# A two-layer three-mixer trunk: another order of the projections, and neighbouring query blocks paired in the weights-by-values products

## The chip, the cores and the metric

The kernel runs on one core of a Trainium2 chip, in one launch. The time is the device time of one execution in microseconds (us), the median of several. The engines are named as in the profile: PE is TensorE's matrix multiplication, PEld its loading of weights, DVE is VectorE, ACT is ScalarE, POOL is GpSimd and SP is SyncE, which here issues most DMAs.

## The reference

The input is 512 rows of 1024 values, ahead of which 16 learned meta rows are set, so 528 positions. Two layers follow, and each does this (cut to what matters):

```python
h = rmsnorm(x) ; proj = h @ w_in        # about 8400 columns, split into the inputs below
# A: stick-breaking attention, 8 heads of 64
# B: latent attention, 8 heads: q and k from low-rank codes, softmax, v of 64
# C: differential attention, 4 heads: (softmax1 - lam * softmax2) @ v, v of 128, then RMSNorm
y_sb, y_mla, y_diff = [(o * silu(z)) @ w_o for each branch]
merged = sum(sigmoid(gate logits) * y for the three branches)
x = x + merged @ w_out
```

Softmax is taken in query blocks of 128 positions. In B and C block j sees the keys of blocks 0 to j and 64 more, in A a query sees the keys before it. After the second layer comes a last RMSNorm, and the meta rows are dropped.

## The kernel before, in words

All products are done with float32 operands split in a high and a low part of a faster 4-byte type (H and L): one product is three matmuls, H by H, H by L and L by H (`mm3`, line 408). So nearly each operand passes a split: ACT copies the high part (line 430), DVE subtracts it (line 435, `low`), and PE waits for both.

The program is laid out at build time by a planner in the kernel (`Builder`). Each piece of work is a task, a Python generator that tells the engine of its next step; the planner keeps a planned time for each engine, takes the step that can start first, and writes its instructions down. The chip then runs each engine's instructions in that order: an engine that waits holds back everything written behind it. The projections, which make up most of PE's work, are one task of lowest priority (`products`): it goes through a list of items in a fixed sequence, and the attention's tasks are written down between its matmuls. An item can start when its weights are split and its condition holds; most conditions ask for memory (`room`).

The sequence is a string per layer, `ORDER`. Its letters: Q, q, k are the projections of A's queries and keys, V its values; C are B's codes; D i is the query and key projection of head i of C (two items, `dqk_item`, each with a rotation on DVE), U its values (`v_item`, item names dv); W and M are B's values and queries and keys; x, y, z are the gated paths of A, C, B; g and G are gate logits that are computed early and parked in DRAM (tensor g_d); s, m, d are the output projections of the branches A, B, C, where each `y` item (`y_item`) loads two parked gate logits from g_d and adds to a running sum in DRAM (acc_d), which the first two branches store and the last two load. `load_x` and `wo_items` close the layer: the product with w_out.

Memory is one pool of 33 double pages. An item that finds too few pages free waits, and with it all items behind it.

The softmax of a head of B or C runs as blocks j = 3, 2, 1, 0 and, in layer 0, -1 for the meta rows (`sm_block`). A block is: scores on PE (`z`, shapes of 264, 400, 272, 144 columns), maximum on DVE (lines 1155 and 1157), exponential with a sum on ACT, reciprocal, and normalising on DVE (for C a TENSOR_SCALAR of line 444 and a SCALAR_TENSOR_TENSOR of line 439), transposition on PE (line 414, one matmul per key block), split by ACT and DVE into the slabs H and L. When all blocks of a head of C are there, `diff_av` does weights by values; for B `mla_av` does it for two heads and two of the four blocks at a time. In both, a pair of query blocks that needs the same key block is one step of 256 columns, and a block that needs a key block alone is one of 128. Blocks are paired as 0 with 2 and 1 with 3.

Of the kernel before, what the change touches and what calls it, by code (L numbers as in the profile page):

```python
# [18 lines left out]
T = 528  # L19
META = 16  # L20
# [10 lines left out]
HOP = dict(T=190.0, A=110.0, V=290.0, S=100.0, G=150.0)  # L31
PE_LATE = 100.0
ORDER = (
    "Q0 G14 G15 G00 V0 q1 g23 G27 k1 g26 C0 g05 Q2 V1 g13 Q3 g20 g22 g21 U0 D0 D1 U1 g16 D2 g24 x0 g01 D3 g25 g03 g17 g06 g07 W0 g12 M0 x2 x1 s9 g02 x3 s0 M1 y0 s1 g04 M2 s2 y1 W1 g10 z1 y3 M3 m9 d9 y2 z0 d2 s3 z2 g11 z3 m3 d1 d0 m2 m1 m0 d3",
    "Q0 G15 V0 G03 q1 G27 G23 k1 g26 Q2 C0 g05 V1 g22 g13 Q3 g21 g20 U0 D0 g12 D1 U1 g16 D2 g01 g24 g14 x0 g07 D3 g00 x2 g17 W0 M0 g25 x1 s9 x3 g02 g06 s0 M1 s1 g04 s3 s2 M2 z0 z2 W1 y0 y1 z3 M3 d9 y2 g10 y3 g11 z1 m9 d2 m3 d0 m2 m1 m0 d1 d3",
)
SB_AHEAD = 3
FINE = 80
# [316 lines left out]
class Builder:  # L355
# [765 lines left out]
    def sm_block(self, st, j):  # L1121

        nc = self.nc
        l, kind = st["l"], st["kind"]
# [59 lines left out]
        if kind == "d":  # L1184
            yield "T", both(lambda: st.get("ptfree"), lambda: self.P.can(2 if j == 3 else 1) if self.o_used == 0 else None)
            self.o_used += 1
            tb = self.P.alloc(2 if j == 3 else 1)
            tf = tb.flat()
            self.transposes(tf, P[0], j)
            P[0].free()  # L1190
            H, L = [s[j % 2].flat()[:, 416 if j > 1 else 0:][:, 0:w] for s in st["pt"]]
            yield from self.split(H, L, tf[:, 0:w])
            tb.free()
            self.o_used -= 1
            self.sm_left(st)
            return
        e, at = j % 2, 416 if j > 1 else 0
        for us in [(0, 1)] if j < 3 else [(0,), (1,)]:
            yield "T", both(lambda: self.P.can(2) if self.o_used == 0 else None, lambda: self.R.can(*[2, 2] * sum((e, u) not in st for u in us)))
            self.o_used += 1  # L1200
            tb = self.P.alloc(2)
            for i, u in enumerate(us):
                if (e, u) not in st:
                    st[e, u] = (self.R.alloc(2), self.R.alloc(2))
                self.transposes(tb.flat()[:, 512 * i:], P[u], j)
                P[u].free()
            left = Latch(len(us), lambda: (tb.free(), self.o_free()))
            for i, u in enumerate(us):
                H, L = [s.flat()[:, at:at + w] for s in st[e, u]]
                self.spawn(self.sm_turned(st, e, H, L, tb.flat()[:, 512 * i:512 * i + w], left), f"m{l}{st['u']}{j}")  # L1210

    def o_free(self):
        self.o_used -= 1

    def sm_turned(self, st, e, H, L, src, left):
        yield from self.split(H, L, src)
        left()
        st["n", e] = st.get(("n", e), 0) + 1
        if st["n", e] == 4:
            self.spawn(self.mla_av(st, e), f"m{st['l']}{st['u']}{e}")  # L1220

    def mla_av(self, st, e):

        yield "T", lambda: self.P.can(1)
        ps = self.P.alloc(1, True)
        for u in range(2):
            h = st["u"] * 2 + u
            vo = 128 * (h % 4)
            o = ps.v()[:, 256 * u:256 * u + 256].rearrange("p (a n) -> p a n", n=128)
            for bi in range(e + 4):  # L1230
                v = st["V"][h // 4][bi].v()
                H, L = [s.flat() for s in st[e, u]]
                if bi < e + 2:
                    H, L = [t[:, 0:832].rearrange("p (a n) -> p a n", n=416)[:, :, 128 * bi:128 * bi + 128] for t in (H, L)]
                    self.mm(o, v[:, vo:vo + 128], H, bi == 0 and u == 0, False)
                    self.mm(o[0:64], v[:, vo:vo + 64], L, False, False)
                else:
                    H, L = [t[:, 416 + 128 * bi:544 + 128 * bi] for t in (H, L)]
                    self.mm3(o[0:64, 1], v[:, vo:vo + 64], v[:, vo + 64:vo + 128], H, L, False, bi == e + 3)
        for u in range(2):  # L1240
            for s in st[e, u]:
                s.free()
        od = st["oslab"].v()
        q = [od[64 * u:64 * u + 64, META:T].rearrange("p (a b n) -> p b a n", b=2, n=128)[:, e] for u in range(2)]
        o = [ps.v()[:, 256 * u:256 * u + 256].rearrange("p (a n) -> p a n", n=128) for u in range(2)]
# [65 lines left out]
    def diff_av(self, st):  # L1311
# [3 lines left out]
        ps = self.P.alloc(1, True)  # L1315
        V = st["V"][h // 2]
        vo = 128 * (h % 2)
        pv = ps.v().rearrange("p (a b n) -> p b a n", b=2, n=128)
        for bi in range(5):
            j0 = max(0, bi - 1)  # L1320
            v = V[bi].v()
            for u in (0, 1):
                a0 = 0 if u >= j0 else 1
                if u + 2 < j0:
                    continue
                H, L = [t[u].flat()[:, 0:1056] for t in st["pt"]]
                if a0 == 0:
                    H, L = [t[:, 0:832].rearrange("p (a n) -> p a n", n=416)[:, :, 128 * bi:128 * bi + 128] for t in (H, L)]
                else:
                    H, L = [t[:, 416 + 128 * bi:544 + 128 * bi] for t in (H, L)]  # L1330
                self.mm3(pv[:, u, :, :] if a0 == 0 else pv[:, u, 1, :], v[:, vo:vo + 128], v[:, 256 + vo:256 + vo + 128],
                         H, L, bi == 0 and u == 0, bi == 4)
        st["ptdone"]()
        parts = st["slabs"][0]
        for s in st["slabs"][1:]:
# [11 lines left out]
        for a2, b2 in self.qr(l):  # L1347
            m = b2 - a2
# [854 lines left out]
```

## Time and profile before

| what | us |
|---|---|
| median of 3 runs (1365.02 to 1368.45) | 1368.17 |
| the profiled execution, its own time | 1365.92 |
| its span, first to last instruction | 1364.2 |
| PE busy | 1325.5 |
| DVE busy | 1002.8 |
| ACT busy | 831.2 |

PE is busy for 97% of the span, with 9506 matmuls, so time is lost or won where PE idles and in the number and width of its matmuls. A matmul's own duration in the profile (some 280 ns for 256 columns) overlaps with its neighbours'; what one costs in a stream is the distance from one start to the next. The mean granted clock of PE is 0.991 of 2.4 GHz.

### The profile page before, as it was taken

What the parts mean: (1) busy time and instruction counts of PE and PEld (TensorE: products, weight loads), DVE (VectorE), ACT (ScalarE), POOL (GpSimd) and SP (SyncE); (2) the same over time, 40 slices, a digit from 0 to 9 for tenths busy, and PEclk for the clock granted to TensorE, in tenths of its full rate; (3) what the DMA queues carried; (4) which work ended last, traced back from release to release, by engine and by line L of the source; (5) the groups of instructions that cost most, each with busy time, mean ns of one, the idle gap of its engine ahead of it and who ended that gap; (6) DMA issues with size and microseconds to landing.
All of it is one profiled execution on the core that took longest, in us unless ns stands there. A gap on an engine that the chain in (4) does not pass through costs nothing.

```text
span 1364.2 us, 25553 instructions
## 1 busy us (share of the span) xinstructions
PE 1325.5 (97%) x9506; PEld 1234.8 (91%) x9506; DVE 1002.8 (74%) x2318; ACT 831.2 (61%) x2003; POOL 111.4 (8%) x232
## 2 busy tenths in 40 slices
PE   9999999969999999999999999999999999999996
PEld 8999999969999999999998889898888888888886
DVE  7877866787776776857776678577977867676664
ACT  6678688555665665645557587574645656455352
POOL 0111012000000102000001120020000110110000
PEclk9999999989999999999999999999999999999998
DMA  4431323313233434248733423233242345423861
GB/s 156 127 116 59 116 75 108 104 48 93 80 115 116 122 106 128 74 163 303 230 110 102 117 74 103 94 93 117 63 131 83 108 122 173 127 79 108 288 236 63
DMA packets 67613, 164.73 MB, mean 121 GB/s; under 512 B 8792, under 2 KB 15320, under 8 KB 67488
## 3 DMA queue, kind: packets, MB, share of 16 engines
q1 hardware_dynamic: 59488, 149.21, 33.5%
q0 software_dynamic: 7168, 13.12, 4.7%
q8 instruction: 75, 1.23, 0.4%
q10 hardware_dynamic: 832, 0.76, 0.2%
q14 instruction: 50, 0.41, 0.1%
HBM read 124.39 MB, written 25.56 MB: 110 GB/s over the span
## 4 chain that ended last, share of the span: by engine, by line
PE 83%; DVE 9%; ACT 4%; DMA 2%; issue 1%; SPq 0%; POOL 0%; DVEq 0%; ACTq 0%; POOLq 0%
PE banks L405 80%; ACT page L430 4%; DVE page L435 4%; PE banks L414 3%; DVE page L439 2%; DVE wl L435 1%; DMA wr<-in_ws_dram 1%; ACT wh L430 1%; DMA page<-page 0%; DVE mx L1157 0%; DVE mx L1155 0%; DMA page<-g_d 0%; DVE page L444 0%; DVE page L449 0%; SPq L457 0%
## 5 line engine op out<-in xcount | busy, mean ns | idle before, releaser
L405 PE MATMUL banks<-hH,wh 128*128 128x256 f32 (+3 forms) x1272 | 402.3, 317 | 0.0
L405 PE MATMUL banks<-hL,wh 128*128 128x256 f32 (+3 forms) x1272 | 396.9, 313 | 0.0
L405 PE MATMUL banks<-hH,wl 128*128 128x256 f32 (+2 forms) x1240 | 388.9, 314 | 0.0
L405 PE MATMUL banks<-page,wh 128*128 128x256 f32 (+2 forms) x1708 | 357.4, 306 | 1.1 <-ACT wh L430 1.0
L430 ACT ACTIVATE wh<-wr 128x256 fp32r<-128x256 f32 (+2 forms) x524 | 237.4, 487 | 144.0 <-PE banks L405 102.2
L430 ACT ACTIVATE page<-page 128x272 fp32r<-128x272 f32 (+19 forms) x486 | 248.5, 531 | 115.3 <-DVE page L435 76.5
L430 ACT ACTIVATE page<-banks 128x272 f32<-128x272 f32 (+21 forms) x493 | 224.1, 465 | 155.2 <-PE banks L405 114.7
L435 DVE TENSOR_TENSOR wl<-wr,wh 128x256 fp32r<-128x256 f32 (+2 forms) x522 | 260.8, 516 | 57.8 <-ACT wh L430 55.1
L405 PEld LDWEIGHTS banks<-page,wh 128*128 128x128 f32 x1708 | 276.9, 190 | 15.4 <-ACT wh L430 2.1
L435 DVE TENSOR_TENSOR page<-page,page 128x256 f32<-128x256 f32 (+15 forms) x429 | 232.8, 558 | 63.7 <-ACT page L430 51.1
L405 PE MATMUL banks<-page,wl 128*128 128x256 f32 (+2 forms) x854 | 260.5, 305 | 1.7 <-DVE wl L435 1.7
L405 PEld LDWEIGHTS banks<-hH,wh 128*128 128x128 f32 (+1 forms) x1272 | 237.4, 187 | 13.1
L405 PEld LDWEIGHTS banks<-hL,wh 128*128 128x128 f32 (+1 forms) x1272 | 237.0, 186 | 12.2
L405 PEld LDWEIGHTS banks<-hH,wl 128*128 128x128 f32 x1240 | 233.5, 188 | 14.4
L405 PE MATMUL banks<-page,page 128*128 128x256 f32 (+17 forms) x1369 | 186.0, 275 | 11.1 <-DVE page L435 4.9
L405 PEld LDWEIGHTS banks<-page,page 128*128 128x128 f32 (+5 forms) x1369 | 161.0, 167 | 24.0 <-DVE page L435 7.3
L405 PEld LDWEIGHTS banks<-page,wl 128*128 128x128 f32 x854 | 161.9, 190 | 9.4 <-DVE wl L435 2.8
L435 DVE TENSOR_TENSOR page<-banks,page 128x256 fp32r<-128x256 f32 (+11 forms) x262 | 125.3, 492 | 31.1 <-ACT page L430 19.7
L457 POOL DMA_DIRECT2D page<-page x112 | 57.5, 518 | 766.9 <-issue 203.9
L430 ACT ACTIVATE page<-banks,mx 128x400 f32<-128x400 f32 (+4 forms) x144 | 71.9, 508 | 35.3 <-DVE mx L1157 18.2
L439 DVE SCALAR_TENSOR_TENSOR page<-page,banks 128x256 f32<-128x256 f32 (+1 forms) x108 | 54.5, 511 | 38.5 <-ACT page L430 27.8
L435 DVE TENSOR_TENSOR page<-page,banks 64x256 f32<-64x256 f32 (+6 forms) x90 | 41.9, 470 | 52.0 <-ACT page L430 26.4
(81 smaller groups left out, 1245.4 us busy)
## 6 DMA issues: line engine op xcount, KB each, us to landing
wr<-in_ws_dram SPq DMA_DIRECT2D x173, 512.0 KB, 3.7
g_d<-page SPq DMA_DIRECT2D x24, 264.0 KB, 2.3
page<-g_d SPq DMA_DIRECT2D x24, 264.0 KB, 4.1
g_d<-page SPq DMA_DIRECT2D x24, 256.0 KB, 2.1
page<-g_d SPq DMA_DIRECT2D x24, 256.0 KB, 4.7
page<-page POOLq DMA_DIRECT2D x20, 264.0 KB, 3.7
acc_d<-page SPq DMA_DIRECT2D x16, 264.0 KB, 2.9
page<-acc_d SPq DMA_DIRECT2D x16, 264.0 KB, 5.3
```

Source lines behind the costliest of these rows:

```text
L405: self.nc.tensor.matmul(out, lhsT, rhs, start=start, stop=stop, skip_group_check=True)
L414: self.nc.tensor.transpose(out, in_, self.idf[0:in_.shape[0], 0:in_.shape[0]])
L430: self.nc.scalar.activation(out=out, in_=in_, func=func, scale=scale, **kw)
L435: self.nc.vector.tensor_tensor(out=out, in0=a, in1=b, op=op)
L439: self.nc.vector.scalar_tensor_tensor(out=out, in0=a, scalar=s, in1=b, op0=op0, op1=op1)
L457: (self.nc.gpsimd if pool else self.nc.sync).dma_start(out=out, in_=in_)
```

## The change

Three things change. The two strings of `ORDER` are laid out anew; among much else, the early gate logit g20 of layer 0 moves from before U0 to between D0 and D1, and the output projections at the end of both layers stand in another sequence. Query blocks are paired 0 with 1 and 2 with 3 in `diff_av` and `mla_av`, so block 3's weights, of five key blocks, no longer fit beside its partner's in one slab and are split in two pieces; B's blocks are taken in the sequence 3, 2, 1, 0 instead of 3, 1, 2, 0. The reserve of memory that `room` keeps for a softmax yet to start grows by one single page.

```diff
 ORDER = (
-    "Q0 G14 G15 G00 V0 q1 g23 G27 k1 g26 C0 g05 Q2 V1 g13 Q3 g20 g22 g21 U0 D0 D1 U1 g16 D2 g24 x0 g01 D3 g25 ...
+    "Q0 G14 G15 G00 V0 q1 g23 k1 G27 C0 Q2 g05 V1 g26 Q3 g22 g13 g21 U0 D0 g20 D1 U1 g16 x0 D2 g01 g24 D3 g25 ...
...
-                two, one_f = two + 2, one_f + 5
+                two, one_r, one_f = two + 2, one_r + 1, one_f + 5
...
-        more = [2] * (4 if kind == "m" and j > 1 else 0)
+        more = [2] * (4 if kind == "m" and j % 2 == 1 else 0)
...
+            if j == 3:
+
+                H, L = [s[0].flat()[:, 256:384] for s in st["pt"]]
+                yield from self.split(H, L, tf[:, 512:640])
...
-    def sm_turned(self, st, e, H, L, src, left):
-        yield from self.split(H, L, src)
+    def sm_turned(self, st, e, parts, left):
+        for H, L, src in parts:
+            yield from self.split(H, L, src)
...
-            for bi in range(e + 4):
+            for bi in range(2 * e + 3):
...
-                if bi < e + 2:
+                if bi < 2 * e + 2:
...
-        js = ((3, 2, 1, 0) if st["kind"] == "d" else (3, 1, 2, 0)) + ((-1,) if st["l"] == 0 else ())
+        js = (3, 2, 1, 0) + ((-1,) if st["l"] == 0 else ())
...
-                if u + 2 < j0:
+                if 2 * u + 1 < j0:
                     continue
```

First place, PE in layer 0, where the scores and transpositions of the first head of C meet the projections. A matmul that reads hH, hL, wh, wl is a projection; one that reads two pages is attention's; L414 is a transposition. Before, from the last matmuls of the item dk of head 1 on (144 columns are the scores of block 0, 16 of block -1, 264 of block 3 of the second head):

```order
L405 MATMUL banks<-hH,wl 128x272
L405 MATMUL banks<-page_3043,page_3237 128x144
L405 MATMUL banks<-page_3239,page_3238 128x144
L405 MATMUL banks<-page_3043,page_3237 128x144
L405 MATMUL banks<-page_3239,page_3238 128x144
L414 MATMUL banks<-idf,page_3478 128x128 x5
L405 MATMUL banks<-page_3043,page_3237 16x16
L405 MATMUL banks<-page_3239,page_3238 16x16
L405 MATMUL banks<-page_3043,page_3237 16x16
L405 MATMUL banks<-page_3239,page_3238 16x16
L414 MATMUL banks<-idf,page_3499 128x128 x4
L405 MATMUL banks<-page_3239,page_3401 128x264
```

The same place now, from the last of the first head's scores to the first transposition and on:

```order
L405 MATMUL banks<-hH,wl 128x256
L405 MATMUL banks<-hH,wh 128x256
L405 MATMUL banks<-hL,wh 128x256
L405 MATMUL banks<-hH,wl 128x256
L405 MATMUL banks<-hH,wh 128x272
L405 MATMUL banks<-hL,wh 128x272
L405 MATMUL banks<-hH,wl 128x272
L405 MATMUL banks<-hH,wh 128x272
L405 MATMUL banks<-hL,wh 128x272
L405 MATMUL banks<-hH,wl 128x272
L414 MATMUL banks<-idf,page_3409 128x128 x5
L405 MATMUL banks<-hH,wh 128x272
```

Before, the transpositions x5 (block 3) come right behind the scores, and 33 more rows of attention alone follow until the next projection. Now the scores stand inside the item dq of head 1, and projections follow the transpositions at once.

DVE at the same place, from the first head's first maximum to the end of block 3's normalising. Before it took 20 rows (they begin with a memset of 64x64 and two maxima of line 1155); the last twelve of them read:

```order
L435 TENSOR_TENSOR page_3479<-banks,page_536 128x256
L439 SCALAR_TENSOR_TENSOR page_3401<-page_3404,page_3401 128x272
L435 TENSOR_TENSOR page_3499<-page_3499,page_1690 128x256
L1169 RECIPROCAL rs<-sm 128x2
L1151 MEMSET banks 64x2x64
L1157 TENSOR_REDUCE mx<-banks 128x2
L439 SCALAR_TENSOR_TENSOR page_3402<-page_3404,page_3402 64x272
L435 TENSOR_TENSOR page_3479<-page_3479,page_3499 128x256
L435 TENSOR_TENSOR wl<-wr,wh 128x256
L444 TENSOR_SCALAR page_3479<-page_3479,rs,lamn 128x528
L449 STREAM_SHUFFLE page_3499<-banks 128x272
L439 SCALAR_TENSOR_TENSOR page_3478<-page_3478,rs,page_3479 128x528
```

And now, all of it:

```order
L1151 MEMSET banks 64x64 x2
L1155 TENSOR_REDUCE mx<-banks 128x1 x2
L435 TENSOR_TENSOR wl<-wr,wh 128x256 x2
L1151 MEMSET banks 64x2x64
L1157 TENSOR_REDUCE mx<-banks 128x2
L1169 RECIPROCAL rs<-sm 128x2
L1151 MEMSET banks 64x2x64
L1157 TENSOR_REDUCE mx<-banks 128x2
L444 TENSOR_SCALAR page_3409<-page_3409,rs,lamn 128x528
L1151 MEMSET banks 64x2x64
L1157 TENSOR_REDUCE mx<-banks 128x2
L439 SCALAR_TENSOR_TENSOR page_3409<-page_3409,rs 128x528
```

The shuffles, additions and multiplications of the rotation (L449 and L435 with pages) that stood between are gone from here; the maxima of blocks 2, 1 and 0 stand in it instead.

Second place, SP at the end of layer 1: weights (wr), stores and loads of the running sum (acc_d), gate logits (g_d). Before, up to the last loads ahead of w_out:

```order
L457 DMA wr<-in_ws_dram 128x1024
L457 DMA acc_d<-page_14968 128x512
L457 DMA page_14965<-g_d 128x512
L457 DMA acc_d<-page_14968 128x512
L457 DMA wr<-in_ws_dram 128x1024
L457 DMA page_14965<-g_d 128x512
L457 DMA page_15028<-acc_d 128x512 x2
L457 DMA page_15060<-g_d 128x512 x2
L457 DMA page_15063<-acc_d 128x512 x2
L457 DMA wr<-in_ws_dram 128x1024
L457 DMA page_15112<-g_d 128x512 x2
L457 DMA page_15115<-acc_d 128x512 x2
```

And now:

```order
L457 DMA page_14938<-g_d 128x512 x2
L457 DMA page_14941<-acc_d 128x512 x2
L457 DMA acc_d<-page_14905 128x512 x2
L457 DMA wr<-in_ws_dram 128x1024
L457 DMA page_14984<-g_d 128x512 x2
L457 DMA page_14987<-acc_d 128x512 x2
L457 DMA wr<-in_ws_dram 128x1024
L457 DMA page_15036<-g_d 128x512 x2
L457 DMA page_15039<-acc_d 128x512 x2
L457 DMA wr<-in_ws_dram 128x1024
L457 DMA page_15086<-g_d 128x512 x2
L457 DMA page_15089<-acc_d 128x512 x2
```

Before, the last two stores are those of the fourth-last y item, and a g_d load of the item after it stands between them. Now the last two belong to the fifth-last y item, the loads of the item after it stand ahead of them, and none stands between.

## Rows read from the trace of the kernel before

**Rows 1.** The page, part 1: busy time of PE (share of the span).
```profile
PE 1325.5 (97%) x9506; PEld 1234.8 (91%) x9506; DVE 1002.8 (74%) x2318; ACT 831.2 (61%) x2003; POOL 111.4 (8%) x232
```

**Rows 2.** Windows: length, busy (count) of PE, PEld, DVE, ACT, POOL, PE clock, DMA.
```profile
0.00:40.00 40.00, 35.15 (x244) 32.06 (x245) 30.68 (x83) 25.82 (x65) 3.03 (x10) 1.00 0.55 173
265.00:275.00 10.00, 10.00 (x79) 9.79 (x79) 9.77 (x29) 5.04 (x14) 0.51 (x1) 1.00 0.18 57
275.00:294.30 19.30, 8.16 (x53) 6.99 (x51) 18.00 (x51) 11.56 (x39) 1.04 (x2) 0.73 0.31 84
1296.00:1308.00 12.00, 9.67 (x49) 8.18 (x49) 9.33 (x16) 7.40 (x13) 0.00 (x0) 0.92 0.78 275
1320.00:1364.20 44.20, 33.47 (x275) 32.71 (x273) 23.16 (x51) 15.11 (x32) 0.00 (x0) 0.92 0.25 84
```

**Rows 3.** Timeline of PE around the idle stretch: start, length, work, idle before.
```profile
267.80 0.29 PE L405 MATMUL banks<-page,page 128*128 128x264 f32 x1
...
268.04 0.28 PE L405 MATMUL banks<-hL,wh 128*128 128x256 f32 x1
...
270.65 0.28 PE L405 MATMUL banks<-hH,wl 128*128 128x256 f32 x1
...
275.00 0.56 PE L405 MATMUL banks<-page,page 128*128 128x144 f32 x4
...
278.17 0.77 PE L414 MATMUL banks<-idf,page 128*128 128x128 f32 x5 [2.60 <-ACT wh L430]
...
285.82 1.11 PE L414 MATMUL banks<-idf,page 128*128 128x128 f32 x4 [6.16 <-DVE page L439]
...
294.29 0.36 PE L405 MATMUL banks<-wh,hH 128*128 128x256 f32 x1
```

**Rows 4.** Timeline of DVE, softmax of the first differential head, four blocks.
```profile
269.21 0.19 DVE L1151 MEMSET banks<- 64x64 f32 x2
...
269.36 1.32 DVE L1155 TENSOR_REDUCE mx<-banks 128x1 f32<-128x528 f32 x2
...
274.27 0.99 DVE L1157 TENSOR_REDUCE mx<-banks 128x2 f32<-128x800 f32 x1
...
276.10 0.42 DVE L435 TENSOR_TENSOR wl<-wr,wh 128x256 fp32r<-128x256 f32 x1
...
276.44 0.55 DVE L444 TENSOR_SCALAR page<-page,rs,lamn 128x528 f32<-128x528 f32 x1
...
277.26 0.76 DVE L439 SCALAR_TENSOR_TENSOR page<-page,rs,page 128x528 f32<-128x528 f32 x1
...
283.43 0.72 DVE L1157 TENSOR_REDUCE mx<-banks 128x2 f32<-128x544 f32 x1
...
284.77 0.46 DVE L1157 TENSOR_REDUCE mx<-banks 128x2 f32<-128x288 f32 x1
```

**Rows 5.** Timeline of PE: weights-by-values product of one differential head, layer 0.
```profile
358.75 3.22 PE L405 MATMUL banks<-page,page 128*128 128x256 f32 x27
361.81 0.34 PE L405 MATMUL banks<-hH,wh 128*128 128x272 f32 x1
```

**Rows 6.** Timeline of PE: the same product of a latent-attention pair, layer 1.
```profile
1203.30 2.45 PE L405 MATMUL banks<-page,page 128*128 128x256 f32 x24
1205.59 0.62 PE L414 MATMUL banks<-idf,page 128*128 128x128 f32 x4
```

**Rows 7.** Timeline of SP (DMA issues) and, last, ACT, end of layer 1.
```profile
1289.60 0.32 SPq L457 DMA_DIRECT2D acc_d<-page  x1
...
1289.97 0.42 SPq L457 DMA_DIRECT2D page<-g_d  x1
...
1294.17 0.72 ACT L430 ACTIVATE page<-page,bg 128x512 f32<-128x512 f32 x1 [5.28 <-DMA page<-g_d]
```

**Rows 8.** Groups of ACT and DVE by shape: count, busy, mean ns of one.
```profile
L430 ACT ACTIVATE page<-banks 128x256 fp32r<-128x256 f32 x66 | 24.1, 379 | 17.4 <-PE banks L405 11.6 <-PE banks L414 5.1
...
L435 DVE TENSOR_TENSOR page<-banks,page 128x256 fp32r<-128x256 f32 x64 | 25.7, 417 | 10.3 <-ACT page L430 9.8
```

More of the change, by code (lines that the diff above doesn't have):

```diff
@@ L1190, in sm_block @@
             P[0].free()
-            H, L = [s[j % 2].flat()[:, 416 if j > 1 else 0:][:, 0:w] for s in st["pt"]]
-            yield from self.split(H, L, tf[:, 0:w])
+            n, at = min(w, 512), 512 * (j % 2)
+            H, L = [s[j // 2].flat()[:, at:at + n] for s in st["pt"]]
+            yield from self.split(H, L, tf[:, 0:n])
+            if j == 3:
+                H, L = [s[0].flat()[:, 256:384] for s in st["pt"]]
+                yield from self.split(H, L, tf[:, 512:640])
             tb.free()
@@ L1196, in sm_block @@
             return
-        e, at = j % 2, 416 if j > 1 else 0
+        e, at, n = j // 2, 512 * (j % 2), min(w, 512)
         for us in [(0, 1)] if j < 3 else [(0,), (1,)]:
-            yield "T", both(lambda: self.P.can(2) if self.o_used == 0 else None, lambda: self.R.can(*[2, 2] * sum((e, u) not in st for u in us)))
+            one = [1] * (j == 3 and "end" not in st)
+            yield "T", both(lambda: self.P.can(2) if self.o_used == 0 else None, lambda: self.R.can(*[2, 2] * sum((e, u) not in st for u in us), *one))
             self.o_used += 1
@@ L1206, in sm_block @@
                 P[u].free()
+            if one:
+                st["end"] = self.R.alloc()
             left = Latch(len(us), lambda: (tb.free(), self.o_free()))
             for i, u in enumerate(us):
-                H, L = [s.flat()[:, at:at + w] for s in st[e, u]]
-                self.spawn(self.sm_turned(st, e, H, L, tb.flat()[:, 512 * i:512 * i + w], left), f"m{l}{st['u']}{j}")
+                parts = [[s.flat()[:, at:at + n] for s in st[e, u]] + [tb.flat()[:, 512 * i:512 * i + n]]]
+                if j == 3:
+                    parts.append([st["end"].v()[:, 256 * u + 128 * k:256 * u + 128 * k + 128] for k in range(2)] + [tb.flat()[:, 512:640]])
+                self.spawn(self.sm_turned(st, e, parts, left), f"m{l}{st['u']}{j}")
     def o_free(self):
         self.o_used -= 1
-    def sm_turned(self, st, e, H, L, src, left):
-        yield from self.split(H, L, src)
+    def sm_turned(self, st, e, parts, left):
+        for H, L, src in parts:
+            yield from self.split(H, L, src)
         left()
@@ L1237, in mla_av @@
                 else:
[L1238 to L1242, printed above, removed]
+                    if e:
+                        H, L = [st["end"].v()[:, 256 * u + 128 * k:256 * u + 128 * k + 128] for k in range(2)]
+                    else:
+                        H, L = [t[:, 768:896] for t in (H, L)]
+                    self.mm3(o[0:64, 1], v[:, vo:vo + 64], v[:, vo + 64:vo + 128], H, L, False, True)
+        for s in [s for u in range(2) for s in st[e, u]] + [st["end"]] * e:
+            s.free()
         od = st["oslab"].v()
-        q = [od[64 * u:64 * u + 64, META:T].rearrange("p (a b n) -> p b a n", b=2, n=128)[:, e] for u in range(2)]
-        o = [ps.v()[:, 256 * u:256 * u + 256].rearrange("p (a n) -> p a n", n=128) for u in range(2)]
+        q = [od[64 * u:64 * u + 64, META + 256 * e:META + 256 * e + 256] for u in range(2)]
+        o = [ps.v()[:, 256 * u:256 * u + 256] for u in range(2)]
         yield "A", None
@@ L1322, in diff_av @@
             for u in (0, 1):
-                a0 = 0 if u >= j0 else 1
-                if u + 2 < j0:
+                o = ps.v()[:, 256 * u:256 * u + 256]
+                if 2 * u + 1 < j0:
                     continue
-                H, L = [t[u].flat()[:, 0:1056] for t in st["pt"]]
-                if a0 == 0:
-                    H, L = [t[:, 0:832].rearrange("p (a n) -> p a n", n=416)[:, :, 128 * bi:128 * bi + 128] for t in (H, L)]
-                else:
-                    H, L = [t[:, 416 + 128 * bi:544 + 128 * bi] for t in (H, L)]
-                self.mm3(pv[:, u, :, :] if a0 == 0 else pv[:, u, 1, :], v[:, vo:vo + 128], v[:, 256 + vo:256 + vo + 128],
-                         H, L, bi == 0 and u == 0, bi == 4)
+                H, L = [t[u].flat() for t in st["pt"]]
+                if 2 * u >= j0:
+                    o = o.rearrange("p (a n) -> p a n", n=128)
+                    H, L = [t[:, 0:1024].rearrange("p (a n) -> p a n", n=512)[:, :, 128 * bi:128 * bi + 128] for t in (H, L)]
+                else:
+                    o = o[:, 128:256]
+                    H, L = [t[:, 768:896] for t in (H, L)] if u == 0 else [t[0].flat()[:, 256:384] for t in st["pt"]]
+                self.mm3(o, v[:, vo:vo + 128], v[:, 256 + vo:256 + vo + 128], H, L, bi == 0 and u == 0, bi == 4)
         st["ptdone"]()
```

7 lines of the change are left out of this document (3 added, 4 removed).

## The prediction

> **What bounds the kernel now.** I read the page first: PE is busy for 1325.5 of 1364.2 us [rows 1], so all that can be won is PE's idle time, 38.7 us, and the cost of its matmuls. Next the windows, to find where the idle time lies: start 40.00 - 35.15 = 4.85 us, end 44.20 - 33.47 = 10.73, the 19.3 us from 275.00 to 294.30 with 19.30 - 8.16 = 11.14, the change to the output projection with 2.33; the rest, 9.7 us, is spread thin [rows 1, 2]. So one place holds more idle time than any other that a schedule could reach.
>
> The timeline of PE tells what happens there. From 275.00 to 294.29 no projection runs: PE gives out four scores, waits 2.60 us for the first transpositions, later 6.16 us for the next ones, and takes the following item, dv of C, only at 294.29 [rows 3]. All 53 matmuls of the stretch are attention's. DVE meanwhile is busy for 18.00 of 19.30 us, and had been for 9.77 of the 10 us before [rows 2]: it was full of the rotations of two heads when the first softmax came, and the softmax's steps stood between them. Two things thus met: a chain through a full DVE, and nothing on PE to lay over it. That nothing was written there is the planner's doing: dv asks for five single pages and a reserve, and its condition held only when the blocks of the first two heads had handed theirs back. The granted clock fell to a mean of 0.73 there, so part ran at 1.2 instead of 2.4 GHz; it was 1.00 in the 10 us before [rows 2].
>
> What would the 53 matmuls take without a wait? From 268.04 to 270.65 lie 22 steps of 256 columns, 0.119 us each [rows 3]. Eight of 264, four of 400, four of 272 and eight of 144 columns are 5952 columns, 2.8 us; fourteen transpositions at 0.108 (below) are 1.5; the small ones some 0.7. Together 5.0 us. The stretch loses 19.3 - 5.0 = 14.3 us, 11.14 in idle time and 3.2 by the lower clock.
>
> **The change part by part.** *Pairing.* Number of columns and of products stay; where a key block served two lone blocks of 128 columns, it now serves more pairs. For a head of C the lone matmuls fall from 12 to 6 and the pairs' rise from 15 to 18. The 27 of before take 361.81 - 358.75 = 3.06 us [rows 5]; 15 at 0.119 are 1.78, so a lone one costs 1.28 / 12 = 0.107. Now 18 x 0.119 + 6 x 0.107 = 2.78: 0.28 saved, for 8 heads 2.2 us. For two heads of B, both halves together, lone matmuls fall from 24 to 12, pairs' rise from 20 to 24. One half (12 and 12) took 1205.59 - 1203.30 = 2.29 us [rows 6]: 1.43 for the pairs, 0.86 / 12 = 0.072 for a lone one. Saved: 12 x 0.072 - 4 x 0.119 = 0.39 us, for 8 such units 3.1. A lone one there loads 64 columns of weights, and the transpositions behind the 24 may have waited a little, so as a lower bound I take half of a pair's price, 0.059: 0.23 us, for 8 units 1.9. Pairing gives 4.1 to 5.3 us; I take 4.7.
>
> The Trainium skill ("TensorE: Matmul & The Clock Gate", section on LDWEIGHTS) prices a weight load by its columns, P / 1.2 ns, 107 ns for 128 and 53 for 64. The lone matmul of C at 0.107 agrees with that: it is bound by its weights, not by its 128 columns. By the same rule the lone one of B is not bound by weights, which speaks for its lower bound, and the sum would be 4.1 instead of 4.7.
>
> *The extra splits.* Block 3 is split in two pieces: 8 heads of C and 16 of B, 24 more instructions on ACT and 24 on DVE, of at most 0.38 and 0.42 us (rows of 256 columns, where these have 128) [rows 8]. On PE's path that would be up to 24 x 0.80 = 19 us. I take nothing: block 3 is the first of its head, the product waits for the last, and three blocks' work lies between; DVE idles for 26% of the span [rows 1].
>
> *The first softmax of C.* Now g20 lies between the two heads' projections, so DVE meets the rotations of the second head later, and dv no longer waits for memory: no item of projections is held while attention runs alone. The order of PE shows the longest run without a projection as some 5 us of work, with projections behind each wait. But one wait should remain. Between block 3's scores and its transpositions PE now has 30 projection matmuls (24 of 256 and 6 of 272 columns) and 16 scores: 24 x 0.119 + 6 x 0.126 + 1.8 = 5.4 us. DVE's rows for that chain are now twelve: 0.19 + 1.32 for block 3's maxima, two weight pieces at 0.42, the maxima of blocks 2, 1 and 0 with 0.99, 0.72 and 0.46, then 0.55 and 0.76 to normalise, and about 0.4 for memsets and a reciprocal [rows 4], 6.2 us; with two hand-overs of some 0.3 us, 6.8. So PE waits 1.4 us where it waited 2.60 and 6.16. Bounds: none, if DVE's work overlaps at its ends, and 4.9 us, if it takes as long as before (the last score begins at 267.80, the transpositions at 278.17, 10.3 us) [rows 3]. What is late next are the transpositions of block 2, which by the same prices have 7.4 us of PE work ahead of them; a chain no longer than block 3's is covered.
>
> *The end of layer 1.* Before, ACT waited 5.28 us for a parked gate logit, whose load stood on SP behind a store of the running sum that was itself late [rows 7]; the weights of the output projection, converted on ACT behind that, came late, PE idled for 2.33 us and its clock fell to a mean of 0.92 over 12 us [rows 2], worth another 0.08 x 12 = 1.0 us. Now the last stores stand one item earlier and no load stands between them. Whether that is enough the order doesn't tell: between 0 and 3.3 us, I take 2.0.
>
> *All else that is moved.* The sequence of both layers changes in many places, with the same items and DMAs. The spread idle time of 9.7 us will fall otherwise. Rows of the program up to the first 40 us and those behind w_out stay as they are, so start and end stay. I take 1.0 us of new waits, between -2 and +5.
>
> Sum: -4.7 - 14.3 + 1.4 - 2.0 + 1.0 = -18.6 us, against 1365.92 us of the profiled execution 1347.3. That execution lies 2.25 us under the median of the runs shown, so I forecast 1368.17 - 18.6 = 1349.6, say 1350.
>
> **Rivals.** *The wait moves along.* If the first head's two waits, 2.60 and 6.16 us, both recur because DVE is still behind, the clock falls again for 3.2 us, and the end of layer 1 is as before, then -4.7 - 14.3 + 8.8 + 3.2 + 1.0 = -6.0: 1362. For it speaks that the amount of rotation and softmax work is the same; against it that in the new order of DVE the rotations stand behind the chain instead of in it.
>
> *Slower: each head of C gets such a wait.* Projections of C's heads now lie amid gate logits all through both stages, with DVE at 9.7 of 10 us in such stretches [rows 2]. PE runs in order, so a chain longer than the work laid over it stops all. Eight heads times a wait w for block 3 take the gain back from w = 18.6 / 8 = 2.3 us on, and the kernel is measurably slower above 2.8; at 4.9 us, the upper bound above, it would be 1350 + 8 x 4.9 - 1.4 = 1388. Against it: PE's spread idle time of 9.7 us is all that the other seven heads cost before, together with everything else.
>
> *The pairing doesn't do what it says*, because a lone matmul hid behind something: 1350 + 4.7 = 1354.3. [Rows 5] speak against that for C.
>
> *More is won*: the wait of 1.4 goes, the end is repaired wholly, and the spread waits shrink: -5.3 - 14.3 - 3.3 - 2.0 = -24.9, 1343.3; below that lies only what no row here tells of.
>
> **How the numbers follow.** Forecast with its own bounds (1343 to 1360, from -24.9 to -4.1 - 14.3 + 4.9 + 5.0 = -8.5): 0.78, with the case without a gain from pairing and that of more won within it. The wait moves along, 1360 to 1364: 0.10. Below 1343: 0.03. Slower: 0.05. No measurable change: 0.04. What a measurement tells from no change is about 0.3%, 4.1 us. Faster by more: 0.91, same 0.04, slower 0.05. The range leaves out the cases beyond 1360 and below 1342: 1342 to 1360.
>
> **What the profile of the changed kernel would show.** Some 9418 matmuls on PE, 88 fewer. No window of 19 us with PE under half busy near 275 us, a clock of 1.00 there, and the item dv running through between attention's steps. A wait of 1 to 2 us ahead of the first transpositions x5 of C. The product of a head of C in 2.8 instead of 3.06 us. Around the output projection of layer 1 less than 2.33 us idle. The prediction is wrong if a new stretch without projections appears, if the first transpositions of C wait over 5 us, or if many small waits of PE come up together to more than 15 us.

## The result, and the profile after

The changed kernel takes 1352.09 us (median of 4 runs, 1350.29 to 1353.43), the kernel before beside it 1366.6 (1364.81 to 1368.45): the ratio is 0.9893, 95% interval [0.9871, 0.9915]. By medians 14.5 us are won. The profiled execution took 1353.43 us, its span is 1351.5: 12.7 less than before's 1364.2.

The page of the changed kernel, busy time of each engine, beside [rows 1]:

```profile
PE 1321.1 (98%) x9418; PEld 1229.7 (91%) x9418; DVE 1008.9 (75%) x2350; ACT 829.9 (61%) x2019; POOL 111.9 (8%) x232
```

88 matmuls fewer, and 1351.5 - 1321.1 = 30.4 us of idle time on PE for 38.7. Windows of the changed kernel (columns as in [rows 2]): the start, 30 us around the first softmax of C, the end of layer 1.

```profile
0.00:40.00 40.00, 33.82 (x242) 31.32 (x242) 30.17 (x82) 25.56 (x64) 3.03 (x10) 0.99 0.56 173
260.00:270.00 10.00, 8.07 (x62) 7.68 (x61) 7.67 (x21) 5.15 (x15) 0.00 (x0) 1.00 0.65 171
270.00:280.00 10.00, 10.00 (x87) 9.86 (x86) 9.92 (x33) 6.62 (x25) 0.00 (x0) 1.00 0.06 25
280.00:290.00 10.00, 9.01 (x76) 8.78 (x75) 9.61 (x30) 5.21 (x14) 1.02 (x2) 1.00 0.43 108
1280.00:1292.00 12.00, 12.00 (x54) 9.69 (x53) 10.30 (x18) 8.24 (x15) 0.00 (x0) 1.00 0.86 292
```

The half-empty stretch is gone: where 275.00 to 294.30 had 8.16 us of work at a mean clock of 0.73, PE now is busy for 27.08 of 30 us at 1.00. At the end of layer 1 PE doesn't idle at all. The start, though, lost 1.3 us of busy time in the same 40 us.

PE's timeline around the first softmax of C: scores of block 3 and, in the same group of eleven, of block 2; of block 1 (272); of block 0 (144); then the first transpositions.

```profile
263.40 0.28 PE L405 MATMUL banks<-page,page 128*128 128x264 f32 x1
264.62 1.82 PE L405 MATMUL banks<-page,page 128*128 128x264 f32 x11 [0.94 <-DMA page<-page]
...
268.14 0.77 PE L405 MATMUL banks<-page,page 128*128 128x272 f32 x4 [1.00 <-ACT page L430]
...
269.46 0.56 PE L405 MATMUL banks<-page,page 128*128 128x144 f32 x4
...
272.27 0.71 PE L414 MATMUL banks<-idf,page 128*128 128x128 f32 x5
```

DVE at the same place, beginning and end of block 3's chain:

```profile
265.67 0.24 DVE L1151 MEMSET banks<- 64x64 f32 x2 [0.68 <-PE banks L405]
265.82 1.31 DVE L1155 TENSOR_REDUCE mx<-banks 128x1 f32<-128x528 f32 x2
...
271.08 0.76 DVE L439 SCALAR_TENSOR_TENSOR page<-page,rs 128x528 f32<-128x528 f32 x1
```

The chain on DVE lasts from 265.67 to 271.84, 6.17 us, where 6.2 were worked out. The transpositions don't wait. PE's waits fall on the scores instead: 0.94 for a page that a DMA on POOL copies, 1.00 for one that ACT hands back.

The products of weights and values, a head of C in layer 0 and a half of two heads of B in layer 1, with what follows:

```profile
361.88 2.93 PE L405 MATMUL banks<-page,page 128*128 128x256 f32 x24
364.64 0.34 PE L405 MATMUL banks<-hH,wh 128*128 128x272 f32 x1
...
1201.05 2.45 PE L405 MATMUL banks<-page,page 128*128 128x256 f32 x22
1203.34 0.62 PE L414 MATMUL banks<-idf,page 128*128 128x128 f32 x4
```

A head of C takes 364.64 - 361.88 = 2.76 us for 3.06 [rows 5]. The half of B has 16 pairs and 6 lone matmuls in 2.29 us: (2.29 - 16 x 0.119) / 6 = 0.064 for a lone one.

**Where the time went.** To compare whole kernels I price each matmul by the distance to the next one in an unbroken stream (256 columns 0.118 us, 272 0.125, 512 0.232, a lone 128 with 128 weight columns 0.11, and so on), and subtract the sum from the distance between starts. What is left is lost to waits and to the lower clock. The priced work is 1291.6 us before and 1287.2 after. The places are given in us of priced work, so that they mean the same in each kernel; in the trace they come later, by up to 70 us at the end of layer 1.

| lost, us, in the profiled execution | start (0 to 40) | first heads of C (200 to 280) | other heads of C (280 to 380) | B, layer 0 (380 to 510) | end of layer 1 (1220 to 1260) | elsewhere |
|---|---|---|---|---|---|---|
| before | 13.3 | 15.7 | 3.6 | 4.1 | 4.3 | 20.0 |
| after | 14.8 | 4.7 | 4.4 | 6.3 | 0.1 | 22.5 |
| e1_g20_only | 12.0 | 11.1 | 3.2 | 4.1 | 5.5 | 21.1 |
| e2_after_g20_back | 12.6 | 16.5 | 3.2 | 7.4 | -0.1 | 20.3 |
| e3_pair_only | 13.3 | 18.6 | 3.6 | 16.7 | 4.1 | 21.6 |
| e4_end_back | 12.7 | 4.1 | 4.4 | 8.3 | 0.9 | 21.5 |
| e5_order_only | 14.1 | 3.9 | 11.0 | 6.2 | 0.0 | 20.0 |
| e6_no_reserve | 13.4 | 3.8 | 10.6 | 2.1 | 5.2 | 23.5 |
| e7_pair_late | 13.8 | 18.5 | 3.4 | 12.5 | 5.8 | 24.0 |
| e8_after_late | 15.4 | 4.1 | 10.3 | 8.7 | 1.3 | 17.6 |
| e9_end1_only | 13.5 | 18.0 | 3.6 | 4.1 | 1.5 | 20.1 |
| e10_new0_old1 | 12.7 | 4.0 | 4.4 | 7.8 | 4.1 | 24.5 |
| e11_old0_new1 | 12.0 | 18.5 | 3.5 | 16.7 | -0.2 | 21.4 |
| e12_pair_c | 15.0 | 18.5 | 3.5 | 14.8 | 4.2 | 18.1 |

Before to after: 4.4 of work, 11.0 at the first heads of C and 4.2 at the end of layer 1 are won, 19.6; given back are 1.5 at the start, 0.8, 2.2 and 2.5, together 7.0. That leaves 12.6, within 0.1 of the difference of the spans.

The kernels after, e4 and e10 run the same program through layer 0, and yet they show 12.7 to 14.8 at the start and 6.3 to 8.3 in B's stage. Terms below some 2 us can't be read from one execution; what follows rests on larger ones, or on the ratios. At the start the rows show what differs: behind a wait of PE near 39 us the granted clock of the next 10 us is 0.83 in the kernel before, 0.66 in the changed one and 1.00 in e4, which runs the changed kernel's instructions there (rows in this order, columns as above):

```profile
39.00:49.00 10.00, 9.63 (x72) 9.66 (x73) 9.54 (x27) 6.58 (x21) 0.00 (x0) 0.83 0.31 110
39.00:49.00 10.00, 9.28 (x59) 9.31 (x60) 8.44 (x24) 6.60 (x21) 0.00 (x0) 0.66 0.25 84
39.00:49.00 10.00, 9.63 (x77) 8.89 (x78) 9.68 (x28) 6.99 (x22) 0.00 (x0) 1.00 0.31 113
```

### The profile page after: what moved, and what is told of

Same layout as the page of the kernel before. It is cut to its first block, busy times and chain, and to the rows that moved or that the text cites. A ratio compares the mean times of both kernels' runs of the same rounds, so it can differ in the third digit from the quotient of the medians.

```text
span 1351.5 us, 25418 instructions
## 1 busy us (share of the span) xinstructions
PE 1321.1 (98%) x9418; PEld 1229.7 (91%) x9418; DVE 1008.9 (75%) x2350; ACT 829.9 (61%) x2019; POOL 111.9 (8%) x232
## 5 line engine op out<-in xcount | busy, mean ns | idle before, releaser
L405 PE MATMUL banks<-hH,wh 128*128 128x256 f32 (+4 forms) x1272 | 403.7, 318 | 0.2 <-ACT page L430 0.2
L405 PE MATMUL banks<-hL,wh 128*128 128x256 f32 (+4 forms) x1272 | 396.9, 313 | 0.0
L430 ACT ACTIVATE page<-page 128x272 fp32r<-128x272 f32 (+17 forms) x486 | 248.8, 531 | 108.1 <-DVE page L435 70.8
L430 ACT ACTIVATE page<-banks 128x512 fp32r<-128x512 f32 (+21 forms) x509 | 222.8, 450 | 145.8 <-PE banks L405 108.9
L435 DVE TENSOR_TENSOR wl<-wr,wh 128x256 fp32r<-128x256 f32 (+4 forms) x522 | 261.4, 517 | 45.6 <-ACT wh L430 43.2
L405 PEld LDWEIGHTS banks<-page,wh 128*128 128x128 f32 x1708 | 276.0, 190 | 14.3 <-ACT wh L430 1.5
L435 DVE TENSOR_TENSOR page<-page,page 128x256 f32<-128x256 f32 (+16 forms) x429 | 232.5, 558 | 61.3 <-ACT page L430 47.1
L405 PEld LDWEIGHTS banks<-hH,wh 128*128 128x128 f32 (+1 forms) x1272 | 237.5, 187 | 13.4 <-ACT page L430 0.3
L405 PE MATMUL banks<-page,page 128*128 128x256 f32 (+18 forms) x1266 | 178.5, 279 | 9.9 <-DMA page<-page 3.3
L405 PEld LDWEIGHTS banks<-page,page 128*128 128x128 f32 (+5 forms) x1266 | 154.8, 169 | 23.2 <-ACT page L430 5.2
L435 DVE TENSOR_TENSOR page<-banks,page 128x256 fp32r<-128x256 f32 (+10 forms) x286 | 128.4, 463 | 34.6 <-ACT page L430 24.3
L435 DVE TENSOR_TENSOR page<-page,banks 64x256 f32<-64x256 f32 (+6 forms) x90 | 41.9, 470 | 51.8 <-PE banks L405 29.6
```

What stands on the lines that cost most here:

```text
L405: self.nc.tensor.matmul(out, lhsT, rhs, start=start, stop=stop, skip_group_check=True)
L430: self.nc.scalar.activation(out=out, in_=in_, func=func, scale=scale, **kw)
L435: self.nc.vector.tensor_tensor(out=out, in0=a, in1=b, op=op)
```

## The experiments

My theory was the prediction's own: g20's place frees the stretch, pairing saves its matmuls, the last stores free the end of layer 1, and the rest costs little. Each run undoes one of these, or does one alone. Ratios are to the kernel before, with their 95% intervals.

**e1_g20_only.** The kernel before, with g20 alone moved to between D0 and D1:

```diff
-... Q3 g20 g22 g21 U0 D0 D1 U1 ...
+... Q3 g22 g21 U0 D0 g20 D1 U1 ...
```

> The kernel before with one word of its sequence moved: g20 of layer 0 from ahead of U0 to between D0 and D1; pairing and all else as before. My theory (most of the gain is the idle stretch of the first softmax of C, which g20 covers): 11 to 14 us less than before, ratio 0.990 to 0.992, no window near 275 us with PE under half busy. Rival (the stall only moves along, or the gain comes from the sum of many small moves): 0 to 4 us less, ratio 0.997 to 1.000.

Measured: 1361.75 us, 0.9955 [0.9939, 0.9971]. About half of what was expected. PE's waits in this stretch:

```profile
243.78 0.49 PE L405 MATMUL banks<-page,page 128*128 128x512 f32 x1 [1.72 <-ACT page L430]
245.04 0.91 PE L405 MATMUL banks<-page,page 128*64 128x512 f32 x3 [0.77 <-DVE page L435]
...
266.74 0.94 PE L405 MATMUL banks<-page,page 128*128 128x144 f32 x8 [0.89 <-ACT page L430]
269.77 0.38 PE L405 MATMUL banks<-hH,wh 128*128 128x256 f32 x1 [2.09 <-DVE page L444]
```

The waits of 2.60 and 6.16 us [rows 3] are gone, so the move does what the prediction says. But two new pairs of waits come up, one at the last product of A's attention and one in head 1's projection, and the place still loses 11.1 us of 15.7.

**e2_after_g20_back.** The changed kernel with only g20 set back to ahead of U0.

```diff
-... V1 g26 Q3 g22 g13 g21 U0 D0 g20 D1 ...
+... V1 g26 Q3 g22 g13 g21 g20 U0 D0 D1 ...
```

> The changed kernel with g20 set back ahead of U0, all other moves and the pairing kept. My theory: the stretch without projections is back and costs 10 to 13 us more than the changed kernel, so 1362 to 1365, ratio to before 0.997 to 0.999. Rival (many small moves): 1352 to 1355, ratio 0.989 to 0.992.

Measured: 1361.58 us, 0.9955 [0.9938, 0.9972], 9.5 us more than the changed kernel, somewhat less than expected, and the two waits are back, in other sizes:

```profile
281.89 1.33 PE L414 MATMUL banks<-idf,page 128*128 128x128 f32 x5 [5.20 <-DVE page L439]
285.56 1.09 PE L414 MATMUL banks<-idf,page 128*128 128x128 f32 x4 [2.24 <-ACT page L430]
```

So g20's place accounts for two thirds of the whole gain in the changed kernel, 9.5 of 14.5 us; alone in the old sequence it gave some 6 (e1).

**e3_pair_only.** The kernel before with the pairing and its reserve, both strings of `ORDER` left as they were: all of the change but the strings.

> The changed kernel with both strings of the sequence as before, so the pairing alone. My theory: the first softmax's stretch and the late weights at the end of layer 1 stay, 88 matmuls fewer give 4.1 to 5.3 us, ratio 0.996 to 0.997. Rival (a lone matmul hides behind something, or the extra splits eat it): within 1 us, ratio 0.999 to 1.001.

Measured: 1375.17 us, 1.0054 [1.0037, 1.0071]. Slower, though the priced work fell by 4.4 us as it should. B's stage in layer 0 loses 16.7 us for 4.1. The waits at B's first scores are 1.49 and 2.86 us, those quoted at e12 within 0.02.

**e4_end_back.** The changed kernel with the sequence of before for the last output projections of layer 1.

```diff
-... y2 y3 m1 g11 d2 m0 m3 d0 d1 m2 d3
+... y2 y3 g11 d2 m3 d0 m2 m1 m0 d1 d3
```

> The changed kernel with the last output projections of layer 1 in the sequence of before (d2 m3 d0 m2 m1 m0 d1 d3, the running sum's last stores one item later). My theory: PE idles again ahead of the output projection, 2 to 4 us more than the changed kernel, ratio to before 0.991 to 0.993. Rival (the idle time at that place was due to something else): no more than 1 us from the changed kernel, ratio 0.989 to 0.990, and no wait there.

Measured: 1355.34 us, 0.9905 [0.9891, 0.992]. PE loses 0.9 us there, not 4.3. I took this as speaking against the stores; ACT's rows, read beside e9 below, say otherwise. So does the time: the profiled execution, 1352.65 us, is the fastest of its five, and the median lies 3.3 us above the changed kernel's, within the 2 to 4 expected, though the intervals of the two ratios overlap.

**e5_order_only.** The kernel before with both new strings, and neither the pairing nor its reserve.

> The kernel before with both new strings of the sequence, pairing and all else as before: what the order is worth without the pairing. My theory (matmuls saved by the pairing are worth 4.1 to 5.3 us under an order that fits it): 1355 to 1359, ratio to before 0.991 to 0.994. Rival (order and pairing only fit together; without pairing the new order gets waits of its own as the old order got with it): 1362 or more, ratio 0.996 or above.

Measured: 1358.63 us, 0.9942 [0.9925, 0.9959], as expected. So pairing, with its one page more of reserve, is worth 1358.63 - 1352.09 = 6.5 us under the new sequence, while under the old one it costs 0.0054 x 1367 = 7.4. Without it the third head of C has a wait that after doesn't have, and the mean granted clock of the 12 us around it is 0.83:

```profile
348.92 1.30 PE L414 MATMUL banks<-idf,page 128*128 128x128 f32 x5 [2.76 <-DVE page L439]
```

```profile
340.00:352.00 12.00, 8.18 (x54) 7.42 (x53) 8.28 (x22) 4.82 (x15) 0.00 (x0) 0.83 0.54 178
```

**e6_no_reserve.** The kernel before with a smaller reserve in `room`, so that dv's condition holds sooner; the sequence stays. Two double and three single pages come off it, for every item that `room` guards and not for dv alone; two single ones of it stay, where the expectation names three.

```diff
-                two, one_f = two + 2, one_f + 5
+                two, one_f = two, one_f + 2
```

> The kernel before with its sequence and pairing; only the memory that an item must leave free for a softmax yet to start is cut from two double and five single pages to three spare single ones, so that dv need not wait for it. My theory (dv was held by its memory condition, and that let PE idle): projections run through the stretch near 275 us, PE busy there for over 80%, 5 to 12 us less than before, ratio 0.991 to 0.996. Rival (the wait comes from DVE's load alone): PE idles as long, only elsewhere, ratio 0.999 to 1.001.

Measured: 1360.25 us, 0.9954 [0.994, 0.9968], as expected. This shows dv's memory condition to be what held the projections back: PE's instructions are those of before up to the scores of block 0, and the first that differ are dv's, right behind these scores. With g20 where it was, the place loses 3.8 us instead of 15.7, and the first transpositions wait 0.79 instead of 2.60:

```profile
276.43 0.33 PE L405 MATMUL banks<-wh,hH 128*128 128x256 f32 x1
...
279.56 0.74 PE L414 MATMUL banks<-idf,page 128*128 128x128 f32 x5 [0.79 <-ACT wh L430]
```

Of these 11.9 us, 7.0 come back at the later heads of C (10.6 for 3.6).

**e7_pair_late** and **e8_after_late.** In e3 and in the changed kernel, B's first scores wait for copies that POOL makes by DMA. Here the planner is told that these copies end 2 us later than it thinks, so that it writes the scores down later. The first line changed is of the copies for A and C, the second of those for B: the delay holds for all three.

```diff
+POOL_LATE = 2000.0
...
-        self.t = max(r, self.t)
+        self.t = max(r, self.t) + POOL_LATE
...
-                    self.t = r
+                    self.t = r + POOL_LATE
```

> The pairing alone under the old sequence, as in the third experiment, with one planned cost changed: POOL's copies of query and key rows are planned to land 2 us later, so B's first scores are written 16 instead of 3.6 us of PE work behind their projection. My theory (pairing alone lost by scores that waited for these copies, not by the pairing's own work): the waits of 1.5 and 2.9 us ahead of the first pair's scores go, 1366 to 1371, ratio 0.999 to 1.003. Rival (the extra splits or the split slabs cost the time): 1374 or more, ratio 1.004 or above.

Measured: 1378.06 us, 1.0077 [1.0059, 1.0095].

> The changed kernel with the same planned cost changed: POOL's copies are planned to land 2 us later. My theory: the waits for these copies at the first scores of C (0.94 us) and of B's first pair (1.5 us) shrink, 0 to 4 us less than the changed kernel, ratio to before 0.987 to 0.989. Rival (any replanning reshuffles waits of that size at random): within 2 us above or below.

Measured: 1356.02 us, 0.992 [0.9902, 0.9938]. Neither came as the theory had it. In e7 the waits at the first scores of B's first two heads are gone, but others come up 25 to 60 us later and the stage still loses 12.5 us. In e8 5.9 us are lost anew at the later heads of C, and the time is 3.9 us above the changed kernel's, outside its rival's range too. Moving these hand-overs by 2 us lays much of the program out anew.

**e9_end1_only.** The kernel before, with the last output projections of layer 1 in another sequence, so that the last stores of the running sum stand one item earlier.

```diff
-... m9 d2 m3 d0 m2 m1 m0 d1 d3
+... m9 d2 m3 d0 m1 m2 d1 m0 d3
```

> The kernel before with three of layer 1's last output projections in another sequence (m1 m2 d1 m0 d3 for m2 m1 m0 d1 d3), so that the last two stores of the running sum stand with the fifth-last item, as in the changed kernel; nothing else differs. Theory: the place of the last stores on SP decides, so the idle time ahead of the last output projections, 4.4 us against priced work in the kernel before, falls under 1 us, and the kernel takes 3 to 4.5 us less than before (ratio 0.9967 to 0.998). Rival: ACT and DVE are late there for a reason further up in layer 1; then 3 to 5 us stay and the ratio is 0.999 to 1.001.

Measured: 1364.52 us, 0.9973 [0.9958, 0.9988]; 1.5 us are lost at this place for 4.3. The time is as the theory has it, what stays at this place somewhat more. ACT's waits for parked gate logits behind those stores, first in e9, then in the changed kernel, then in e4, and last the second of the two in the kernel before, which [rows 7] don't hold:

```profile
1289.25 1.40 ACT L430 ACTIVATE page<-page,bg 128x512 f32<-128x512 f32 x2 [1.11 <-DMA page<-g_d]
...
1295.43 1.39 ACT L430 ACTIVATE page<-page,bg 128x512 f32<-128x512 f32 x2 [0.40 <-DMA page<-g_d]
```

```profile
1283.04 0.72 ACT L430 ACTIVATE page<-page,bg 128x512 f32<-128x512 f32 x1 [0.66 <-DMA page<-g_d]
1285.07 0.72 ACT L430 ACTIVATE page<-page,bg 128x512 f32<-128x512 f32 x1 [1.30 <-DMA page<-g_d]
```

```profile
1283.06 0.72 ACT L430 ACTIVATE page<-page,bg 128x512 f32<-128x512 f32 x1 [4.71 <-DMA page<-g_d]
1285.64 0.72 ACT L430 ACTIVATE page<-page,bg 128x512 f32<-128x512 f32 x1 [1.86 <-DMA page<-g_d]
```

```profile
1297.79 0.72 ACT L430 ACTIVATE page<-page,bg 128x512 f32<-128x512 f32 x1 [2.90 <-DMA page<-g_d]
```

With the stores early, ACT waits 1.3 us or less; with the old sequence 4.71 and 1.86 in e4, as 5.28 [rows 7] and 2.90 before. So the stores' place does set ACT's waits. What PE feels of them hangs on little: in e4 ACT waits 0.57 and 1.04 us less than before, and PE loses 0.9 us instead of 4.3.

**e10_new0_old1** and **e11_old0_new1.** The changed kernel with the string of one layer taken from before: of layer 1 in e10, of layer 0 in e11.

> The changed kernel with the string of layer 1 of before; pairing and the string of layer 0 stay new. Theory: the new string of layer 1 gives the 4.4 us at its end and nothing else, so this takes 3 to 5 us more than the changed kernel: 1355 to 1357 us, ratio to before 0.992 to 0.9935, with 4 to 6 us of idle time at layer 1's end. Rival: with layer 0 and the pairing new the wait at the end does not come up either (the kernel with the old last output projections had 0.9 us there), so 1351 to 1354 us, ratio under 0.991.

Measured: 1356.69 us, 0.9924 [0.9905, 0.9943], with 4.1 us lost at the end of layer 1: the theory's numbers. The new string of layer 1 is worth some 4.6 us, about what its end alone lost.

> The changed kernel with the string of layer 0 of before; pairing and the string of layer 1 stay new. Theory: what pairing lost under the old sequences it lost in layer 0, in the stage of B, so those waits (three slices of 3 to 7 us between 390 and 500 us) and the stretch near 270 us stay, and only the end of layer 1 is won: 1369 to 1372 us, ratio 1.001 to 1.004. Rival: half of the loss lay in layer 1, then 1360 to 1366 us, ratio 0.995 to 0.999.

Measured: 1369.91 us, 1.0016 [1.0003, 1.0029], again the theory's: the loss of e3 lies in layer 0 wholly, 16.7 us in B's stage as there.

**e12_pair_c.** Does pairing lose through B, whose blocks now come in the sequence 3, 2, 1, 0? Here C alone is paired; B, its conditions, the reserve and both strings are those of before. C's share of the extra splits comes with its pairs.

```diff
-            H, L = [s[j % 2].flat()[:, 416 if j > 1 else 0:][:, 0:w] for s in st["pt"]]
-            yield from self.split(H, L, tf[:, 0:w])
+            n, at = min(w, 512), 512 * (j % 2)
+            H, L = [s[j // 2].flat()[:, at:at + n] for s in st["pt"]]
...
```

> The kernel before with blocks 0 and 1, 2 and 3 paired in the products of C alone; B keeps its pairs of 0 with 2 and 1 with 3, its sequence 3, 1, 2, 0 and its conditions, and both strings and the reserve stay as before. Theory: pairing lost under the old sequences through B, whose blocks come in another sequence, so C alone gives its 2.2 us or somewhat less: 1364.5 to 1367.5 us, ratio 0.9975 to 0.9995, with no new waits between 380 and 500 us. Rival: any shift of the planner's times by the shorter products of C ahead of B's stage brings waits there too; then 5 us or more of new waits lie between 380 and 500 us, and the ratio is 1.000 to 1.006.

Measured: 1374.32 us, 1.0041 [1.0025, 1.0058]. The rival's: B's stage loses 14.8 us although nothing in B's own code was touched. First POOL's copies and PE's first scores of B in the kernel before, then the same in e12:

```profile
435.39 2.97 POOL L457 DMA_DIRECT2D page<-page  x6 [33.39 <-ACT page L430]
...
443.96 0.65 PE L405 MATMUL banks<-page,page 100*128 100x264 f32 x4
```

```profile
434.56 2.47 POOL L457 DMA_DIRECT2D page<-page  x5 [0.29 <-DVE page L439]
...
437.01 0.36 PE L405 MATMUL banks<-page,page 100*128 100x264 f32 x1 [1.47 <-DVE page L439]
440.24 1.00 PE L405 MATMUL banks<-page,page 100*128 100x264 f32 x3 [2.87 <-DMA page<-page]
```

The last copy is issued at 435.39 + 2.97 = 438.36 in the first, at 437.03 in the second. In the kernel before the scores stand behind three items of projections, 15.3 us of priced work after B's queries and keys, and begin 5.6 us after the last copy's issue. In e12 the planner has put them behind one item, 3.6 us of work, and PE stands still for 1.47 and 2.87 us. The clock falls there, as over 10 us of e3:

```profile
432.00:442.00 10.00, 5.65 (x34) 5.29 (x33) 3.99 (x12) 3.24 (x7) 2.98 (x6) 0.77 0.34 83
```

In the changed kernel the same scores have 5.7 us of work ahead of them. The last copy is issued at 416.46, the scores begin at that time too, and one wait remains. The profile puts it to DVE. It stands between the first score and the next, as in e12, and the trace's own records speak for the copies: PE's queue stands from 416.48 to 417.96 in the instruction that waits for the last copy, which lands at 417.92, 1.98 us after its issue began at 415.94; in e12 the last copy lands at 440.15, and the next score begins at 440.24.

```profile
413.98 2.48 POOL L457 DMA_DIRECT2D page<-page  x5 [0.54 <-DVE page L439]
...
418.12 1.59 PE L405 MATMUL banks<-page,page 100*128 100x264 f32 x11 [1.30 <-DVE wl L435]
...
page<-page POOLq DMA_DIRECT2D x2, 8.2 KB, 1.9
```

No kernel of these is faster than the changed one; e4 comes nearest, 0.9905 for 0.9893, and the intervals overlap.

## Why the prediction was right, point by point

**The time.** 1352.09 us for 1350, within the range. The gain was put too high: 18.6 us forecast, 14.5 measured by medians. Between the profiled executions it is 12.6: that of the changed kernel is the slowest of its four, 1.3 us above its median, and that of the kernel before lies 0.7 us under the median of its four, 1366.6. That the time comes within 2.1 us of the forecast all the same is in part luck: the 18.6 were taken off 1368.17, the median of three runs.

**Pairing.** Predicted 4.7 us. C: (3.06 - 2.76) x 8 = 2.4; B, with 0.064 for a lone one, (12 x 0.064 - 4 x 0.119) x 8 = 2.3. Together 4.7 of matmul time, as said; by the prices of the table above 4.4. With the same 128 columns a lone one takes 0.107 where it loads 128 columns of weights (C) and 0.064 where it loads 64 (B). The Trainium skill's rule ("TensorE: Matmul & The Clock Gate", section on LDWEIGHTS), 107 and 53 ns for these loads, agrees with the first being bound by its weights, and with the second not. The 4.1 that I worked out by it was low by 0.3 to 0.6: 0.064 lies between the two prices that I had taken for B, 0.059 and 0.072. What the step missed is that these 4.4 us are not a term by themselves: e5 and after give +6.5 for them, e3 gives -7.4. The extra splits show nowhere as a wait that I could single out, but no run has pairs without them.

**The first softmax of C.** Predicted -14.3 + 1.4 = -12.9, measured -11.0. The profiled execution of before lost little for its program: up to the first product of C, to where PE's instructions are the same, it lost 15.2 us at this place, where e3, e11 and e12 lost 16.9 each and e9 17.5. Against those the change wins some 2 us more, about what was forecast. The cause was right: e6 shows the memory condition, e1 and e2 that the two waits go and come with g20's place, and the chain on DVE took 6.17 us for 6.2. That g20's move frees dv by way of this memory is my reading; no run shows that link by itself. The wait ahead of the first transpositions came at another instruction. From the chain's start to the transpositions 272.27 - 265.67 = 6.60 us pass, for the 6.8 worked out, and PE's wait of 1.00 for ACT, at the scores of block 1, lies inside this stretch and takes the place of the 1.4. The 0.94 for the copied page, ahead of the chain, was not foreseen. In sum 4.7 us remain at this place, where 1.4 and the usual thin loss were counted.

**The end of layer 1.** Predicted -2.0 (0 to 3.3), measured -4.2. Mis-sized, since I counted the idle time of one window [rows 2]; the loss at this place was 4.3. e9 shows the stores' place to give 2.8 of it, by the ratio 3.7 us with an interval of 1.6 to 5.7; e10 shows that with the old string all comes back.

**All else that is moved.** Predicted +1.0 (-2 to +5), measured +7.0: the term that was sized worst. 1.5 of it is the start, whose program is the same in e4 and e10, where it lost 12.7: that part is chance. The other 5.5, which by the noise above can't be told from the bound of 5, are small waits, the plainest at B's first scores in layer 0 (6.3 for 4.1). The prediction took waits that a new sequence brings for a small, unordered rest. e12 shows that an edit which shifts the planner's times can bring 10.7 us at a place whose code it doesn't touch (14.8 for 4.1); e5, e6 and e8 have 6 to 7 us of the kind at the later heads of C (10.6 for 3.6 in e6), which their edits reach as well.

**The rivals.** "The wait moves along" did not come at its place, but 7.0 of the 19.6 us were lost elsewhere, 1.5 of them by chance. "Each head of C gets such a wait" holds for one later head, in e5 (11.0 us for 3.6) and not in after. "The pairing doesn't do what it says" is wrong for the matmuls, and true for the time in the old sequence, which I had not thought of. (Its 1354.3 is 1349.6 + 4.7; from the rounded 1350 it would be 1354.7.)

Open stays why the planner puts B's first scores ahead of two items in e12. I read that in the order of the program, and tried no kernel that changes it alone. Pairing C brings shorter products and eight more splits each on ACT and DVE; no run separates the two, and none has the grown reserve alone.

## What to carry to other kernels

In a program whose order is planned ahead and whose engines run in order, the worth of an edit is not its saved work: the same 4.4 us of matmuls were worth 6.5 us under one sequence and cost 7.4 under another, so an edit and a sequence are to be measured together. What can be predicted well is a large wait with a named cause (memory held, a store ahead of a load); the waits that a new layout brings elsewhere can't be left at next to nothing: in this one case they took back 7.0 of 19.6 us, 1.5 of it by chance. Look first at the steps that wait for a copy or another engine with little work laid over: here 3.6 us of work over the copies went with 4.3 us of waits, 5.7 us with 1.3, and 15.3 us with none.

## What the runs showed of the hardware that was not expected

The length of the low clock after a wait differs between executions of the same instructions. Windows of the kernel before and of e9, whose program is the same up to there, behind the same waits of 2.60 and 6.16 us (in e9 they come 1.2 us later):

```profile
288.00:298.00 10.00, 8.09 (x61) 7.35 (x60) 9.34 (x30) 6.02 (x24) 0.53 (x1) 0.95 0.00 0
298.00:304.00 6.00, 6.00 (x50) 5.68 (x50) 3.94 (x11) 4.40 (x11) 0.00 (x0) 1.00 0.01 3
```

```profile
288.00:298.00 10.00, 9.33 (x42) 8.46 (x42) 8.35 (x27) 6.01 (x22) 0.52 (x1) 0.50 0.01 2
298.00:304.00 6.00, 6.00 (x46) 5.83 (x45) 2.86 (x11) 2.58 (x10) 0.00 (x0) 0.85 0.00 0
```

In the first the granted clock is back at 2.4 GHz for most of the 10 us (0.95), in the second it stays at 1.2 GHz for all of them (0.50): PE shows as busy for longer and does fewer matmuls, 42 for 61. With it go 2.3 us more lost at this place (18.0 for 15.7). A stretch with a long wait thus had a price that varied by some 2 us, and one profile shows one draw of it.
